# Down-projection weights of a decoder layer: low parts by accumulating transfers, and in the second feed-forward high parts by casting transfers

## The chip, the cores and the metric

The kernel runs on one core of a Trainium2 chip. The metric is the device time in microseconds (us) of one execution; the median of the runs is compared. TensorE (PE) multiplies matrices, VectorE (DVE), ScalarE (ACT) and GpSimd (POOL) work element by element, SyncE (SP) and GpSimd issue DMA transfers.

## The reference, cut to what matters

A decoder layer for 512 tokens of width 1024: a half-step feed-forward (f1), a mixer with attention and a convolution, a second half-step feed-forward (f2), and a gated embedding. Everything is float32. The part that the change touches is `w_down` of the two feed-forwards, 2816 x 1024 each:

```python
def swiglu(h, w_gu, w_down):
    g, u = jnp.split(h @ w_gu, 2, axis=-1)
    return (jax.nn.silu(g) * u) @ w_down

x = x + 0.5 * swiglu(rmsnorm(x, ffn1_norm[i]), ffn1_wgu[i], ffn1_wdown[i])
... # mixer
x = x + 0.5 * swiglu(rmsnorm(x, ffn2_norm[i]), ffn2_wgu[i], ffn2_wdown[i])
```

## The kernel before, in words

**Split products.** TensorE multiplies in the rounded format fp32r. To keep float32's accuracy, each operand is split into a high part (the value rounded to fp32r) and a low part (what the rounding left out), and `mm3` sums three products: low weight by high data, high by high, high weight by low data, in this order. So the first matmul of a tile reads the low weight part.

**Weight pieces.** `piece` fetches one 128 x 1024 piece of weights (512 KB; 128 x 768 and 384 KB in the last down-projection of each feed-forward): SyncE loads it into a buffer of the class `raw`, ScalarE rounds it into one of the class `hi`, and `split_into` has VectorE (or GpSimd, for some mixer weights) subtract, raw minus high, into one of the class `lo`. There are three buffers of each class (`SLOTS`), shared by all weights of the program.

**A feed-forward.** The 22 blocks of 128 hidden channels (`KF`) are made first plainly (4 of them in f1, 2 in f2: `products`), then in pairs (`pair`). A pair takes seven products of half-width matmuls (256 columns); the weights of some are sums of raw pieces (`f_s`), formed by VectorE or GpSimd. In f1 (`own=True`) the split weights of these sums have buffers of their own; in f2 they take `hi` and `lo` buffers too. The products of a pair stand in the order 1 and 2, 6 and 5, 7 and 3, then 4, each with a g group and a u group of 12 matmuls. After 8, 16 and 22 blocks `down` runs: for each of 8 output tiles one piece of `w_down` and 24 matmuls of 512 columns (18 in the last), then two VectorE operations that scale the tile and add it to x. In the profile the down-projection's tiles are `f_d`, its weights `raw_wd`, `whi_wd` and `wlo_wd`; in the order of instructions `f2_d0_3` is output tile 3 of f2's first down-projection, and `wd2` the weights of f2, `wd1` those of f1.

**What sets the order.** `record` writes the program down as operations without an order between engines. `passes` then lets `simulate`, a planner with a cost for each operation, place them in time, several times over, with the due times that `deadlines` takes from the pass before; `simulate` also gives out the buffers, and may start one of the next ten groups of matmuls (`WINDOW`) when the first in line isn't ready. `hybrid_layer` emits the operations in the order found. On the chip each engine runs its own list strictly in that order, and an instruction whose operands aren't ready, or whose buffer isn't free, holds up all that stand behind it on its engine. GpSimd issues no transfer in the kernel before.

Of the kernel before, what the change touches and what calls it, by code (L numbers as in the profile page):

```python
# [9 lines left out]
F32 = mybir.dt.float32  # L10
F32R = mybir.dt.float32r
I32 = mybir.dt.int32
AF = mybir.ActivationFunctionType
ALU = mybir.AluOpType
AX = mybir.AxisListType

P = 128
# [16 lines left out]
PIECE = 1024  # L34
# [14 lines left out]
MARGIN = 0.0  # L49

CAPS = {"cz": 2, "ct": 4}
FLEX = ("wkv", "wq", "wzc", "wzg", "wap")

class VT:


    def __init__(self, name, shape, dtype, cls):
# [5 lines left out]
        self.late = False  # L65
        self.kind = name[:2] if name[:2] in CAPS else None

# [142 lines left out]

class Op:
    __slots__ = (
        "i eng home flex what a k writes reads cost lat preds succs group ls npred start end vts done lock fset dma outs"
    ).split()


# [10 lines left out]
class Program:  # L227
    def __init__(self):
        self.ops, self.groups, self.tiles = [], [], []
        self.cur = self.behind = None  # L230
        for name, eng in (("tensor", "PE"), ("vector", "DVE"), ("scalar", "ACT"), ("gpsimd", "POOL"), ("sync", "SP"), ("flex", "FLEX")):
            setattr(self, name, Engine(self, eng))
# [13 lines left out]
    def add(self, eng, what, a, k):  # L246
        op = Op()
        op.flex = eng == "FLEX"
        eng = "DVE" if op.flex else eng
# [47 lines left out]
    def costs(self, op, eng=None):  # L297

        ins = op.reads
        o = op.writes[0] if op.writes else None  # L300
        n = max([v.free() for v in ([o] if o else []) + ins])
        psum = any(v.vt.cls == "ps" for v in op.writes + ins)
        eng = eng or op.eng
        op.lock = eng == "POOL"
        op.fset = None
        op.dma = 0.0
        vecs = sum(isinstance(v, V) for v in [*op.a[3:], *(v for n, v in op.k.items() if n != "accum_out")])
        if eng == "PE":
            if op.what == "transpose":
                op.cost, op.lat = 0.112, 0.3  # L310
            else:
                n = op.a[2].free()
                if op.a[2].vt.dtype == F32R:
                    op.cost, op.lat = (0.2272, 0.3) if n > 256 else (0.1197, 0.3)
                else:
                    op.cost, op.lat = max(0.15, n * 0.00167), 0.35
        elif eng == "DVE":
            op.lat = 0.15
            if op.what == "tensor_tensor":
                op.cost = 0.065 + n * 1.055e-3  # L320
            elif op.what == "scalar_tensor_tensor":
                op.cost = 0.08 + n * 1.12e-3
            elif op.what == "tensor_tensor_reduce":
                op.cost = 0.28 + n * 1.02e-3
            elif op.what in ("reduce_sum", "tensor_reduce"):
                op.cost = 0.08 + n * 1.03e-3
            else:
                op.cost = 0.08 + n * (1.25e-3 if psum else 0.9e-3)
            op.lock = not psum and op.what not in ("tensor_tensor_reduce", "reduce_sum", "tensor_reduce", "reciprocal")
        elif op.what == "dma_start" and eng == "ACT":  # L330
            op.cost, op.lat = 0.5, 2.6
        elif eng == "ACT":
            op.cost, op.lat = 0.07 + n * 0.88e-3, 0.17
            op.cost += 0.094 * vecs
            if "accum_out" in op.k:
                op.cost += 0.1
            f = op.a[2].name if len(op.a) > 2 else "Copy"
            op.fset = SETS.get(f)
        elif eng == "POOL":
            op.lat = 0.15  # L340
            if op.what == "tensor_tensor":
                op.cost = 0.14 + n * 2.1e-3
            elif op.what == "tensor_scalar":
                op.cost = 0.25 + n * 0.8e-3
            else:
                op.cost = 0.12 + n * 1.0e-3
        else:
            op.cost, op.lat = 0.47, 0.0
            v = (op.writes + op.reads)[0]
            op.dma = v.free() * v.shape[0] * 4 / 240e3  # L350
# [16 lines left out]
def deadlines(prog, when):  # L367

    end = max(when.values()) + 12.0
    gend = {}  # L370
    for g in prog.groups:
        gend[g] = when[g.ops[-1]] + g.ops[-1].cost
    for op in reversed(prog.ops):
        if op.eng == "PE":
            ls = when[op]
        else:
            ls = end
            for v in op.reads:
                if v.vt.cls == "ps" and not v.vt.name.startswith("cz"):
                    for o, w in op.preds.items():  # L380
                        if o.eng == "PE" and w:
                            ls = min(ls, gend[o.group] + (24.0 if v.vt.late else 5.0))
        for s in op.succs:
            d = s.ls
            if s.preds[op] and not s.eng == op.eng == "PE":
                d -= op.lat + (1.8 + op.dma if op.eng == "SP" else 0.0)
            ls = min(ls, d - op.cost)
        if op.outs and op.outs[0].cls in ("hi", "lo"):
            ls -= MARGIN
        op.ls = ls  # L390


WINDOW = 10


def simulate(prog, slots):

    free = {c: deque(range(n)) for c, n in slots.items()}
    inuse = dict.fromkeys(CAPS, 0)
    ready = {e: [] for e in ENGINES}  # L400
    busy = dict.fromkeys(ENGINES, 0.0)
# [17 lines left out]
    def push(t, kind, x=None):  # L419
        nonlocal seq  # L420
        heapq.heappush(events, (t, seq, kind, x))
        seq += 1
# [7 lines left out]
    dma_free = 0.0  # L430
# [5 lines left out]
    def can(op, slack):  # L436
        for vt in op.outs:
            if vt.slot is None:
                break
        else:  # L440
            return True
        need = {}
        for v in op.writes:
            vt = v.vt
            if vt.slot is None:
                need.setdefault(vt.cls, {})[vt] = True
        for c, vts in need.items():
            spare = 0
            if c == "a":
                if slack > 400.0:  # L450
                    return False
                spare = 0 if slack < 2.0 else 1 if slack < 6 else 3 if slack < 20 else 6
            if slack > LEAD.get(c, 1e9):
                return False
            if len(free[c]) < len(vts) + spare:
                return False
            if any(vt.kind and inuse[vt.kind] >= CAPS[vt.kind] for vt in vts):
                return False
        return True

    def launch(op, t):
        nonlocal dma_free, aset, lock_dve, lock_pool
        for v in op.writes:
            vt = v.vt
            if vt.slot is None:
                vt.slot = free[vt.cls].popleft()
                if vt.kind:
                    inuse[vt.kind] += 1
        c = op.cost
        if op.eng == "ACT" and op.fset and op.fset != aset:  # L470
            c += 1.28
            aset = op.fset
        if op.lock and op.eng == "DVE":
            c += max(0.0, lock_pool - t)
            lock_dve = t + c
        elif op.lock:
            c += max(0.0, lock_dve - t)
            lock_pool = t + c
        op.start = t
        busy[op.eng] = t + c  # L480
        if op.eng == "SP":
            dma_free = max(t + 0.6, dma_free) + op.dma
            op.end = dma_free + 1.5
        else:
            op.end = t + c + op.lat
        push(t + c, "wake")
        push(op.end, "done", op)
        for s in op.succs:
            if s.eng == op.eng != "PE" and s.npred == 1 and s.ls + lag - t < 6.0:
                hold[op.eng] = op.end  # L490
                if op.eng == "DVE" and s.lock:
                    hold["POOL"] = op.end + 0.1
# [4 lines left out]
    def pe(t):  # L497

        nonlocal cur, pos, lag
        while True:  # L500
# [18 lines left out]
            pick = None  # L519
            for n, g in enumerate(pending[:WINDOW]):  # L520
                off, ok = 0.0, True
# [27 lines left out]
    while left:  # L549
# [3 lines left out]
        t = events[0][0]  # L553
        while events and events[0][0] <= t + 1e-9:
            _, _, kind, x = heapq.heappop(events)
# [17 lines left out]
        for e in ENGINES:  # L573
# [29 lines left out]
            op = best[1]  # L603
# [48 lines left out]
def record():  # L652
    nc = Program()
# [41 lines left out]

    def piece(key, i, n=PIECE, off=0, cuts=1):

        raw = nc.tile(f"raw_{key}{i}", [P, PIECE], F32, "raw")
        hi = nc.tile(f"whi_{key}{i}", [P, PIECE], F32R, "hi")
        lo = nc.tile(f"wlo_{key}{i}", [P, PIECE], F32R, "lo")  # L700
        for c in range(cuts):
            s = slice(c * n // cuts, (c + 1) * n // cuts)
            d = slice(off + s.start, off + s.stop)
            nc.sync.dma_start(raw[:, s], Dram(key)[i][:, d])
            split_into(hi[:, s], lo[:, s], raw[:, s], eng=nc.flex if key in FLEX else nc.vector)
        return hi, lo
# [773 lines left out]
    for o in range(KD):  # L1480
# [4 lines left out]
        n = S // 2 if o == KD - 1 else S  # L1485
        for c in range(0, S, n):
            v = slice(c, c + n)
# [134 lines left out]
```

## Time and profile before

| | |
|---|---|
| time, median of 2 runs | 1173.55 us (1172.52 and 1174.57) |
| span of the profiled execution, first to last instruction | 1172.4 us |
| TensorE busy | 1161.6 us, 99% |
| VectorE busy | 973.4 us, 83% |
| ScalarE busy | 639.7 us, 55% |
| GpSimd busy | 456.2 us, 39% |
| granted TensorE clock, mean | 0.999 |
| moved by SyncE's queue | 114.12 MB |

The profile gives the span of one execution. The median of the runs lies 1.1 us above it; the profiled execution's own time beside the span isn't given apart. A row of a group of instructions reads: line, engine, operation, output <- inputs with their shapes, x count, then busy time in us, mean ns of one, and the engine's idle time just before them with what ended it. A row of waits reads: waiting engine and tile <- releasing engine and tile, us in total, times, longest. All operations are emitted by one line, so rows are told apart by the names of tiles.

### The profile page before, as it was taken

The numbers are of one execution on the slowest core, as the hardware profiler recorded it, in microseconds if no ns is written. First come the engines' busy times: TensorE is split into PE (matmuls) and PEld (weight loads), VectorE is DVE, ScalarE is ACT, GpSimd is POOL, SyncE is SP. The second block draws the span as 40 slices with busy tenths as digits, with TensorE's granted clock in tenths as the row PEclk, the third lists the DMA queues.
The fourth block names the chain that finished last, engine by engine and source line by source line (L and its number), as shares of the span: only waits on it lengthen the run. The fifth ranks groups of instructions, "written<-read, shape, count | busy, mean of one in ns | idle before, by whom it ended". The sixth has DMA issues, their size and how long they took to land.

```text
span 1172.4 us, 17962 instructions
## 1 busy us (share of the span) xinstructions
PE 1161.6 (99%) x6740; PEld 1029.6 (88%) x6740; DVE 973.4 (83%) x1481; ACT 639.7 (55%) x1139; POOL 456.2 (39%) x418
## 2 busy tenths in 40 slices
PE   9999999999999999999999999999999999999998
PEld 7898899889988888878888888889988999899886
DVE  8995799679886898999999786678966997599885
ACT  8552455335545579979865573545541555245542
POOL 2430465033303987887898600104402440122000
PEclk9999999999999999999999999999999999999999
DMA  7422323342233221312223233332333223331331
GB/s 226 146 85 96 126 75 106 99 136 76 82 104 100 90 91 37 108 55 72 76 89 106 88 94 93 105 96 102 107 104 132 74 86 100 121 127 41 104 108 72
DMA packets 37815, 115.30 MB, mean 98 GB/s; under 512 B 4704, under 2 KB 9440, under 8 KB 37728
## 3 DMA queue, kind: packets, MB, share of 16 engines
q1 hardware_dynamic: 37584, 114.12, 31.0%
q8 instruction: 53, 0.87, 0.3%
q14 instruction: 34, 0.28, 0.1%
q10 hardware_dynamic: 144, 0.03, 0.0%
HBM read 112.04 MB, written 2.10 MB: 97 GB/s over the span
## 4 chain that ended last, share of the span: by engine, by line
PE 94%; ACT 2%; DVE 2%; POOL 1%; issue 1%; DMA 0%; SPq 0%; DVEq 0%; ACTq 0%
PE f_d L1522 20%; PE ap L1522 4%; PE ga L1522 4%; PE pg L1522 4%; PE cp L1522 4%; PE wo L1522 4%; PE ca L1522 3%; PE gb L1522 3%; PE cb L1522 3%; PE f_u L1522 2%; PE f_g L1522 2%; PE q1b L1522 2%; PE q0b L1522 2%; PE sc L1522 2%; PE f_u14b L1522 1%; PE f_u20b L1522 1%
## 5 line engine op out<-in xcount | busy, mean ns | idle before, releaser
L1522 POOL TENSOR_TENSOR f_s<-raw_wgu,raw_wgu 128x512 f32<-128x512 f32 x51 | 86.6, 1710 | 345.5 <-DMA raw_wgu<-in_wgu 115.6
L1522 POOL TENSOR_TENSOR y<-y,ct 128x507 f32<-128x507 f32 (+27 forms) x90 | 119.1, 1343 | 6.2 <-ACT ct L1522 4.6
L1522 ACT ACTIVATE whi_wgu<-raw_wgu 128x1024 fp32r<-128x1024 f32 (+1 forms) x93 | 76.2, 834 | 81.5 <-PE f_d L1522 29.5
L1522 DVE TENSOR_TENSOR wlo_wgu<-raw_wgu,whi_wgu 128x1024 fp32r<-128x1024 f32 (+1 forms) x93 | 105.1, 1140 | 7.8 <-ACT whi_wgu L1522 7.3
L1522 DVE SCALAR_TENSOR_TENSOR cz<-u,dww,cz 128x504 f32<-128x504 f32 (+25 forms) x145 | 104.7, 732 | 2.3
L1522 ACT ACTIVATE whi_wd<-raw_wd 128x1024 fp32r<-128x1024 f32 (+1 forms) x48 | 47.4, 987 | 103.9 <-PE f_d L1522 84.6
L1522 DVE TENSOR_TENSOR f_d<-f_d,f_n_rb 128x512 f32<-128x512 f32 x48 | 33.4, 697 | 75.8 <-PE f_d L1522 75.8
L1522 DVE TENSOR_TENSOR f_wl<-f_s,f_wh 128x512 fp32r<-128x512 f32 x72 | 71.4, 1012 | 1.5 <-ACT f_wh L1522 1.0
L1522 POOL TENSOR_TENSOR f_s<-raw_wgu,f_s 128x512 f32<-128x512 f32 x31 | 52.3, 1694 | 51.6 <-DVE f_us L1522 20.6
L1522 DVE TENSOR_TENSOR wlo_wgu<-f_s,whi_wgu 128x512 fp32r<-128x512 f32 x80 | 66.3, 863 | 6.0 <-ACT whi_wgu L1522 5.8
L1522 ACT ACTIVATE whi_wgu<-f_s 128x512 fp32r<-128x512 f32 x80 | 46.6, 625 | 32.4 <-PE f_d L1522 8.9
L1522 ACT ACTIVATE ct<-u,dww 128x505 f32<-128x505 f32 (+28 forms) x90 | 58.2, 701 | 2.2 <-DVE u L1522 2.1
L1522 ACT ACTIVATE f_wh<-f_s 128x512 fp32r<-128x512 f32 x72 | 43.6, 626 | 26.6 <-DVE f_s L1522 12.9
L1522 POOL TENSOR_TENSOR f_s<-f_s,raw_wgu 128x512 f32<-128x512 f32 x31 | 49.2, 1594 | 20.8 <-DVE f_s L1522 6.0
L1522 DVE TENSOR_TENSOR wlo_wd<-raw_wd,whi_wd 128x1024 fp32r<-128x1024 f32 (+1 forms) x48 | 54.1, 1128 | 3.8 <-ACT whi_wd L1522 3.6
L1522 ACT ACTIVATE f_gs<-f_gs 128x512 f32<-128x512 f32 x44 | 27.6, 629 | 34.8 <-DVE f_gs L1522 34.4
L1522 POOL TENSOR_TENSOR f_t<-x 128x256 f32<-128x256 f32 x8 | 6.5, 807 | 86.8 <-DVE x L1522 81.6
L1522 DVE SCALAR_TENSOR_TENSOR x<-f_d,x 128x512 f32<-128x512 f32 x48 | 32.9, 689 | 1.4
L1522 DVE TENSOR_TENSOR f_s<-raw_wgu,raw_wgu 128x512 f32<-128x512 f32 x25 | 32.9, 1319 | 0.0
L1522 ACT ACTIVATE s<-s,m,q_r 128x128 f32<-128x128 f32 x64 | 31.0, 491 | 0.5 <-DVE m L1522 0.4
L1522 ACT ACTIVATE whi_wzc<-raw_wzc 128x1024 fp32r<-128x1024 f32 x16 | 17.0, 1061 | 22.3 <-issue 8.4
L1522 ACT ACTIVATE whi_wzg<-raw_wzg 128x1024 fp32r<-128x1024 f32 x16 | 17.1, 1069 | 16.9 <-PE ga L1522 5.0
(1621 smaller groups left out, 4525.3 us busy)
## 6 DMA issues: line engine op xcount, KB each, us to landing
raw_wgu<-in_wgu SPq DMA_DIRECT2D x80, 512.0 KB, 3.7
raw_wd<-in_wd SPq DMA_DIRECT2D x32, 512.0 KB, 3.5
raw_wzc<-in_wzc SPq DMA_DIRECT2D x16, 512.0 KB, 3.6
raw_wzg<-in_wzg SPq DMA_DIRECT2D x16, 512.0 KB, 3.6
raw_wd<-in_wd SPq DMA_DIRECT2D x16, 384.0 KB, 3.1
raw_wgu<-in_wgu SPq DMA_DIRECT2D x32, 128.0 KB, 2.9
raw_wq<-in_wq SPq DMA_DIRECT2D x8, 512.0 KB, 3.6
raw_wap<-in_wap SPq DMA_DIRECT2D x8, 512.0 KB, 3.6
```

The source lines that it names most:

```text
L1522: getattr(engines[op.eng], op.what)(*a, **k)
```

## The change

For the weights of the two down-projections `piece` no longer subtracts. In f1 the piece is loaded and rounded as before; ScalarE then writes the negated high part into the low buffer, and a transfer issued by GpSimd adds the piece from HBM onto it once more, so that low = weight - high. In f2 there is no raw piece: a transfer issued by GpSimd rounds it on the way into the high buffer, and the low part follows as in f1. So a down weight of f2 crosses from HBM twice, both times by GpSimd's queue, one of f1 once by SyncE's and once by GpSimd's. The planner gets a cost for GpSimd's transfers. It also gets a rule for all weights: a piece is given one of the three `hi` (or `lo`) buffers only when it is among the next in the order in which TensorE will use them (`turns`).

```diff
+ADD_ISSUE, ADD_RATE = 1.2, 120e3
+BY_DMA = {"wd1": True, "wd2": False}
...
+        elif eng == "POOL" and op.what == "dma_start":
+            op.cost, op.lat, op.lock = ADD_ISSUE, 0.0, False
+            v = op.writes[0]
+            op.dma = v.free() * v.shape[0] * 4 / (ADD_RATE if "accum_op" in op.k else 240e3)
...
+            if c in TURNS and any(vt not in turns[c][: len(free[c])] for vt in vts):
+                return False
...
+        elif op.dma:
+            dma_free = max(t + c, dma_free) + op.dma
+            op.end = dma_free + 2.0
...
     def piece(key, i, n=PIECE, off=0, cuts=1):
 
+        d = slice(off, off + n)
+        if key in BY_DMA:
+            hi = nc.tile(f"whi_{key}{i}", [P, PIECE], F32R, "hi")
+            lo = nc.tile(f"wlo_{key}{i}", [P, PIECE], F32R, "lo")
+            if BY_DMA[key]:
+                raw = nc.tile(f"raw_{key}{i}", [P, PIECE], F32, "raw")
+                nc.sync.dma_start(raw[:, 0:n], Dram(key)[i][:, d])
+                nc.scalar.activation(hi[:, 0:n], raw[:, 0:n], AF.Copy)
+            else:
+                nc.gpsimd.dma_start(hi[:, 0:n], Dram(key)[i][:, d])
+            nc.scalar.activation(lo[:, 0:n], hi[:, 0:n].bitcast(F32), AF.Copy, scale=-1.0)
+            nc.gpsimd.dma_start(lo[:, 0:n], Dram(key)[i][:, d], accum_op=ALU.add)
+            return hi, lo
```

The planner's order moves with it. Three places follow, all in f2's first down-projection.

On GpSimd, where before only the sums for the next pair (blocks 8 and 9) stood between the sums of block 6 and those of block 10:

```order
L1522 TENSOR_TENSOR f2_s3_6_1_8843<-raw_wgu26_01_8565,f2_s1_6_1_8712 128x512
L1522 TENSOR_TENSOR f2_s0_8_0_9252<-raw_wgu28_10_9224,raw_wgu28_11_9147 128x512
L1522 TENSOR_TENSOR f2_s2_8_0_9265<-raw_wgu28_00_9158,raw_wgu28_10_9224 128x512
L1522 TENSOR_TENSOR f2_s1_8_1_9282<-f2_s0_8_1_9258,raw_wgu28_00_9158 128x512
L1522 TENSOR_TENSOR f2_s3_8_0_9297<-raw_wgu28_01_9191,f2_s1_8_0_9270 128x512
```

Now on GpSimd at the same place (a transfer to `whi` casts, one to `wlo` adds):

```order
L1557 DMA whi_wd20_8995<-in_wd2 128x1024
L1557 DMA whi_wd21_9015<-in_wd2 128x1024
L1557 DMA whi_wd22_9045<-in_wd2 128x1024
L1557 DMA wlo_wd20_9049<-in_wd2 128x1024
L1557 DMA wlo_wd21_9053<-in_wd2 128x1024
L1557 DMA wlo_wd22_9056<-in_wd2 128x1024
L1557 DMA whi_wd23_9088<-in_wd2 128x1024
L1557 DMA whi_wd24_9121<-in_wd2 128x1024
L1557 DMA wlo_wd23_9118<-in_wd2 128x1024
L1557 DMA whi_wd25_9152<-in_wd2 128x1024
L1557 DMA wlo_wd24_9149<-in_wd2 128x1024
L1557 DMA wlo_wd25_9181<-in_wd2 128x1024
```

Twelve transfers have come ahead of the next pair's sums, and the first add stands behind the third cast, the add of piece 3 behind the cast of piece 4.

On ScalarE, before, at the end of the same down-projection and the first weight of the next pair:

```order
L1522 ACTIVATE whi_wd25_9139<-raw_wd25_9059 128x1024
L1522 ACTIVATE whi_wd26_9174<-raw_wd26_9090 128x1024
L1522 ACTIVATE whi_wd27_9207<-raw_wd27_9123 128x1024
L1522 ACTIVATE whi_wgu28_1_9240<-raw_wgu28_00_9158 128x1024
L1522 ACTIVATE whi_wgu28_2_9280<-raw_wgu28_01_9191 128x1024
```

Now on ScalarE, from the negation of piece 4 on:

```order
L1557 ACTIVATE wlo_wd24_9149<-whi_wd24_9121 128x1024
L1557 ACTIVATE wlo_wd25_9181<-whi_wd25_9152 128x1024
L1557 ACTIVATE whi_wgu28_1_9189<-raw_wgu28_00_9106 128x1024
L1557 ACTIVATE whi_wgu28_2_9250<-raw_wgu28_01_9133 128x1024
L1557 ACTIVATE whi_wgu28_6_9301<-f2_s1_8_0_9239 128x512
L1557 ACTIVATE whi_wgu28_6_9301<-f2_s1_8_1_9232 128x512
L1557 ACTIVATE wlo_wd26_9315<-whi_wd26_9271 128x1024
```

Two weights of the next pair have moved ahead of pieces 6 and 7, and stand behind the negation of piece 5.

On TensorE, before, from the end of output tile 3 of this down-projection:

```order
L1522 MATMUL f2_d0_3_9135<-f2_a01h_8820,wlo_wd23_9082 128x512
L1522 MATMUL f2_d0_3_9135<-f2_a01h_8820,whi_wd23_9073 128x512
L1522 MATMUL f2_d0_3_9135<-f2_a01l_8900,whi_wd23_9073 128x512
L1522 MATMUL f2_d0_4_9170<-f2_a00h_8360,wlo_wd24_9115 128x512
L1522 MATMUL f2_d0_4_9170<-f2_a00h_8360,whi_wd24_9106 128x512
```

Now on TensorE at the same place:

```order
L1557 MATMUL f2_d0_3_9156<-f2_a01h_8941,wlo_wd23_9118 128x512
L1557 MATMUL f2_d0_3_9156<-f2_a01h_8941,whi_wd23_9088 128x512
L1557 MATMUL f2_d0_3_9156<-f2_a01l_8958,whi_wd23_9088 128x512
L1557 MATMUL f2_g8b_9194<-f2_h0_h_7767,wlo_wgu28_1_9192 128x256
L1557 MATMUL f2_g8b_9194<-f2_h0_h_7767,whi_wgu28_1_9189 128x256
```

Groups of 12 half-width matmuls of the next pair (`f2_g8b`, `f2_u8b` and others) now stand between output tiles 3 and 4, 4 and 5, and more of them between 5 and 6 and between 6 and 7. f2's second down-projection is arranged like the first. In f1's first two, such groups stand after tile 4, after 5 and after 6 (the group g8a of the pair after the first down-projection comes after tile 5 and one other group). The third down-projection of each feed-forward has none in between.

More of the change, by code (lines that the diff above doesn't have):

```diff
@@ L212 @@
     __slots__ = (
-        "i eng home flex what a k writes reads cost lat preds succs group ls npred start end vts done lock fset dma outs"
+        "i eng home flex what a k writes reads cost lat use preds succs group ls npred start end vts done lock fset dma outs"
     ).split()
@@ L385, in deadlines @@
             if s.preds[op] and not s.eng == op.eng == "PE":
-                d -= op.lat + (1.8 + op.dma if op.eng == "SP" else 0.0)
+                d -= op.lat + (1.8 + op.dma if op.dma else 0.0)
             ls = min(ls, d - op.cost)
@@ L390, in deadlines @@
         op.ls = ls
+        op.use = when[op] if op.eng == "PE" else min((s.use for s in op.succs if s.preds[op]), default=end)
 WINDOW = 10
+TURNS = ('hi', 'lo')
 def simulate(prog, slots):
     free = {c: deque(range(n)) for c, n in slots.items()}
+    first = {}
+    for op in prog.ops:
+        for vt in op.outs:
+            if vt.cls in TURNS and vt not in first:
+                first[vt] = op.use, op.i
+    turns = {c: sorted((k, vt.name, vt) for vt, k in first.items() if vt.cls == c) for c in TURNS}
+    turns = {c: [vt for _, _, vt in ts] for c, ts in turns.items()}
     inuse = dict.fromkeys(CAPS, 0)
@@ L466, in launch @@
                 vt.slot = free[vt.cls].popleft()
+                if vt.cls in TURNS:
+                    turns[vt.cls].remove(vt)
                 if vt.kind:
```

## The prediction

> **What bounds the kernel now.** I read the shares by engine first, then TensorE's waits, then the stretches.
>
> ```profile
> PE 1161.6 (99%) x6740; PEld 1029.6 (88%) x6740; DVE 973.4 (83%) x1481; ACT 639.7 (55%) x1139; POOL 456.2 (39%) x418
> ```
> ```profile
> PE sc L1522 <- DVE qT_l L1522: 2.0, 1, 2.0
> PE warm L1522 <- DVE ones L1522: 1.1, 1, 1.1
> PE f_u L1522 <- ACT f_n_rb L1522: 0.7, 1, 0.7
> PE f_g2a L1522 <- ACT f_gs L1522: 0.6, 1, 0.6
> PE ple_sp L1522 <- DVE ple_dgl L1522: 0.6, 1, 0.6
> PE f_g L1522 <- DVE wlo_wgu L1522: 0.2, 1, 0.2
> PE kTp L1522 <- POOL zk L1522: 0.2, 1, 0.2
> ```
> These are all of TensorE's waits: 5.4 us of 1172.4. No relief of another engine can give back more than that, under 0.5%, and no row names a down-projection. The stretches say the same (f1's first down-projection, its second and third pairs, f2's first and last down-projection; first the stretch and its length, then each engine's busy time):
>
> ```profile
> 93.00:137.00 44.00, 44.00 (x198) 36.50 (x197) 26.24 (x27) 12.58 (x16) 9.30 (x6) 1.00 0.32 104
> 137.00:217.00 80.00, 80.00 (x668) 79.90 (x667) 75.37 (x107) 43.16 (x77) 36.41 (x22) 1.00 0.31 102
> 862.00:906.00 44.00, 44.00 (x199) 36.50 (x198) 27.29 (x31) 9.67 (x11) 6.83 (x4) 1.00 0.44 140
> 1090.00:1123.00 33.00, 33.00 (x149) 27.41 (x148) 28.08 (x40) 17.57 (x25) 0.00 (x0) 1.00 0.42 122
> ```
> TensorE is full in all of them at clock 1.00, though VectorE is at 94% in the second. In the chain that ended last a down-projection is one unbroken piece:
>
> ```profile
> 862.01 43.55 PE f_d L1522 x192
> 1090.54 32.67 PE f_d L1522 x144
> ```
> 43.55 / 192 = 0.227 us a matmul, so an output tile takes 24 x 0.227 = 5.44 us, in the last down-projection 18 x 0.227 = 4.08. The question is only whether the new weight chain can deliver a pair every 5.44 (4.08) us.
>
> **What the change removes.** VectorE loses 48 subtractions:
>
> ```profile
> L1522 ACT ACTIVATE whi_wd<-raw_wd 128x1024 fp32r<-128x1024 f32 x32 | 33.9, 1058 | 86.7 <-PE f_d L1522 84.6 <-PE f_u6b L1522 1.3 <-ACT whi_wd L1522 0.4
> L1522 ACT ACTIVATE whi_wd<-raw_wd 128x768 fp32r<-128x768 f32 x16 | 13.5, 846 | 17.2 <-issue 16.4 <-ACT whi_wd L1522 0.5 <-PE f_u20b L1522 0.2
> L1522 DVE TENSOR_TENSOR wlo_wd<-raw_wd,whi_wd 128x1024 fp32r<-128x1024 f32 x32 | 38.9, 1216 | 2.9 <-ACT whi_wd L1522 2.9
> L1522 DVE TENSOR_TENSOR wlo_wd<-raw_wd,whi_wd 128x768 fp32r<-128x768 f32 x16 | 15.2, 951 | 0.9 <-ACT whi_wd L1522 0.7
> ```
> 38.9 + 15.2 = 54.1 us off VectorE, worth 0 since TensorE never waited there. ScalarE gains 24 negations in f1 (about 1 us each); in f2 they replace the 24 roundings. SyncE loses 24 loads, GpSimd's queue gains 72 transfers. All that is off the path; only latency counts.
>
> **What the new transfers take** stands nowhere in this trace, where GpSimd issues none. The nearest rows are SyncE's loads (size in KB, us from issue to landing):
>
> ```profile
> raw_wd<-in_wd SPq DMA_DIRECT2D x32, 512.0 KB, 3.5
> raw_wd<-in_wd SPq DMA_DIRECT2D x16, 384.0 KB, 3.1
> ```
> 128 KB more cost 0.4 us, so 512 KB are 1.6 us of moving on 1.9 fixed. The *cast* moves as much; I add 1.0 us for GpSimd's issue (its shortest 128x512 add is 1.29 us, in a row below) and take Tc = 4.5 us (4.1 for 384 KB). The *add* also reads its destination: twice the moving, 1.9 + 3.2 + 0.9 = 6.0 = Ta (1.9 + 2.4 + 0.9 = 5.2). Lower end for both: the plain 3.5 and 3.1. Upper end: two us for the issue, and thrice the moving for the add: Tc 5.5 (4.9), Ta 1.9 + 4.8 + 2.0 = 8.7 (7.6). I stay nearer the loads.
>
> The Trainium skill, page "DMA: Bandwidth & Descriptors", section "Anatomy of one DMA — SWDGE (gpsimd) path", fits a GpSimd transfer as 2.0 us + bytes/436e3, an estimate of 3.2 us for 512 KB; with that for both, the sum would be about that of the first rival. No run before this one shows it.
>
> **f2, where the chain lies open.** Three buffers each hold high and low parts, and f2's pairs use the same ones, so a first down weight gets a buffer only when a pair's last products release it (ScalarE, then TensorE's last pair matmul and first down matmul):
>
> ```profile
> 857.94 1.04 ACT L1522 ACTIVATE whi_wd<-raw_wd 128x1024 fp32r<-128x1024 f32 x1
> 859.21 1.06 ACT L1522 ACTIVATE whi_wd<-raw_wd 128x1024 fp32r<-128x1024 f32 x1 [0.23 <-ACT whi_wd L1522]
> 862.20 1.04 ACT L1522 ACTIVATE whi_wd<-raw_wd 128x1024 fp32r<-128x1024 f32 x1
> 867.56 1.06 ACT L1522 ACTIVATE whi_wd<-raw_wd 128x1024 fp32r<-128x1024 f32 x1 [3.46 <-PE f_d L1522]
> ```
> ```profile
> 860.40 0.28 PE L1522 MATMUL f_u6b<-f_t_h,wlo_wgu 128*128 128x256 f32 x1
> ...
> 861.72 0.28 PE L1522 MATMUL f_u6b<-f_t_l,whi_wgu 128*128 128x256 f32 x1
> 861.84 0.40 PE L1522 MATMUL f_d<-f_a00h,wlo_wd 128*128 128x512 f32 x1
> ```
> Buffers came 3.9 and 2.6 us before the first down matmul and 0.4 after it; a tile's release reaches ScalarE 0.2 to 0.3 us after the tile. Today 1.06 + 1.2 us fit. Let E be the time at which the first down matmul would start:
> - Start: cast 0 goes at -3.9, lands at 0.6, its negation ends at 1.8 (two hops of 0.1). On GpSimd the first add stands behind the third cast, which waits for E; it goes at 1.8 and lands at 7.8. The tile's first matmul reads the low part: **7.8 us** of wait.
> - Tiles 0 to 2 run to 24.1. Cast 3 can go when tile 0 is done (13.2), lands at 17.9, is negated at 19.1; its add stands behind cast 4, which waits for tile 1 (18.7) and is issued by 19.7; it lands about 25.4: **1.3 us**. Tile 3 ends at 30.8.
> - TensorE's order then has the next pair's g8b. Its high part stands on ScalarE behind negation 5 (30.0) and takes the buffer that tile 3 frees: 0.2 + 1.06 + 1.2 and hops, **2.7 us**. Add 4 is there by 31, add 5 by 36.
> - Tiles 6 and 7 stand among the pair's products and hold one buffer each through cast, negation and add, so the pair turns over two. A product is 24 x 0.12 = 2.9 us and a new weight about 2.7; where two products are interleaved some 1.3 us are missing. I take **2.0 us** (0 to 7). GpSimd's adds for this pair (next row) wait behind add 5, and are used from tile 5 on; VectorE's freed time covers them. Without that cover, it is one such add, 1.8 us.
>
> ```profile
> L1522 POOL TENSOR_TENSOR f_s<-raw_wgu,raw_wgu x2: 1293/1780/2267, 895.4 to 896.7; 128x512 f32<-128x512 f32 x2
> ```
> That is 13.8 us, twice 27.6. The third down-projection has smaller pieces and no pair to fill in. By the same steps with 4.1, 0.85 and 5.2: 6.4 at the start, 2.4 at tile 3, 2.2 at tile 6, 1.1 at tile 7 (its negation stands behind wgate0's rounding), **12.1 us**.
>
> The third starts like the first two (its first rounding 4.0 us ahead: the first row below, against the last). f1 stands otherwise (the second row; its down-projection starts at 93.0):
>
> ```profile
> 1086.42 0.83 ACT L1522 ACTIVATE whi_wd<-raw_wd 128x768 fp32r<-128x768 f32 x1
> ...
> 77.35 1.06 ACT L1522 ACTIVATE whi_wd<-raw_wd 128x1024 fp32r<-128x1024 f32 x1 [1.01 <-PE f_u6b L1522]
> ```
> ```profile
> 1090.38 0.40 PE L1522 MATMUL f_d<-f_a20h,wlo_wd 128*128 128x512 f32 x1
> ```
> **f1, where it is covered.** The pair's middle weights have buffers of their own, so the first rounding stood 15.6 us ahead. In the stride: tile ends, 0.2 + rounding 1.06 + negation 1.06 + hops 0.2 + Ta 6.0 = 8.5 us, against two tiles = 10.9. The cover goes above Ta = 8.4. What is left is g8a after tile 5 of the first one: its buffer is tile 5's, 2.7 us after it, and one group of 1.4 us lies between: **1.3 us**; in the second a whole tile lies between. The transfer engines have room: 0.32 x 44 = 14 us now, plus 8 adds x 3.2 = 26, gives 40 of 44 us and more.
>
> The mixer's order shifts a little; its waits before sum to 2.8 us (rows sc, ple_sp and kTp), so I put nothing on it.
>
> **The sum**, against the profiled execution's span: 27.6 + 12.1 + 1.3 = 41.0; 1172.4 + 41.0 = 1213.4. The median of the runs lies 1.1 us above the span: **1214.5 us**, 3.5% slower.
>
> **The rivals.**
> 1. *GpSimd's transfers are as short as SyncE's.* Tc = Ta = 3.5 (3.1): 4.4 + 0 + 2.7 + 0 in each of two, 4.6 in the third (3.4 at the start, 1.2 at tile 7), 1.3 in f1: 20.1 us, 1194, which a measurement of 2% can't tell from no change. For it: the same bytes over the same engines, under half busy. Against: an add reads twice. From 41.0 to 20.1 as Tc + Ta falls from 10.5 to 7.0 is 6 us per us; it decides below Tc + Ta = 7.6, where the loss is 23.5 us. Chance 0.17.
> 2. *Adds or issues are slower.* Tc 5.5, Ta 8.7: starts of 11.5, 4.7 at tile 3, 2.7, and 5 in the pair: 23.9 twice; 9.6 + 5.5 + 5.5 in the third; 5 in f1, now past its cover: 73 us, 1247. For it: GpSimd's add above takes 1.29 to 2.27 us for one shape, so something holds that engine up at times. Against: VectorE, which would be the likeliest, is busy for only 27.29 of 44 us there. Chance 0.2. The Trainium skill, page "SBUF — State Buffer", section "SBUF: two separate sides", has a rule that speaks for it: while VectorE runs in a two-port mode, GpSimd can't write a transfer's descriptors. No trace shows it yet.
> 3. *VectorE was the hidden limit*, and 54 us less of it shorten the pair stretches. It would give at most the 5.4 us of waits, 1168. Against: TensorE is at 80.00 of 80.00 there. Chance 0.03.
>
> The forecast has the other 0.6, with its own range 1202 to 1235. The range for 8 in 10 takes in part of both big rivals: 1188 to 1252. Within 2% is 1150 to 1197, what a measurement of this kernel can't tell from no change: 0.18, from rival 1 and what is left of 3; faster by over 2%: 0.01; slower 0.81.
>
> **What would show it.** TensorE's waits list, empty of f_d now, names DMA wlo_wd, most of it at three places, each where f2 passes from pairs to a down-projection, 6 to 10 us a time. f1's down-projections stay within 3 us of 43.55 and 32.67 us. Landing times of whi_wd near 4.5 and of wlo_wd near 6.0 would bear out the sizes. VectorE falls to about 920 us busy with no gain. I am wrong if f2's first down matmul follows the pair within 3 us, or if f1 waits as much as f2.

## The result, and the profile after

The changed kernel takes **1265.48 us** (median of two runs, 1265.32 to 1265.64), 1.0778 times the time before, 95% interval 1.0754 to 1.0801. The forecast was 1214.5 us with a range up to 1252: the direction was right, the time lies outside the range. The profiled execution has a span of 1263.8 us, 91.4 more than before, at a mean granted clock of 0.976. In experiments 9 and 10 one execution took 1.9 and 2.4 times as long as the others; the ratios leave these out.

The shares by engine, after:

```profile
PE 1188.6 (94%) x6740; PEld 1041.9 (82%) x6740; DVE 925.0 (73%) x1424; ACT 665.6 (53%) x1165; POOL 523.9 (41%) x499
```

Start from TensorE, which was at 99%. Its matmuls are the same 6740, so the span's 91.4 us split exactly in two: idle time rose from 10.8 us (1172.4 - 1161.6) to 75.2 (1263.8 - 1188.6), that is by **64.4**, and the *same* matmuls were busy for **27.0** us longer. The forecast had only idle time in its sum, 41.0 us. VectorE is at 925.0 us, 48.4 less, with no gain.

TensorE's waits after (total, times, longest):

```profile
PE f_d L1557 <- DMA wlo_wd<-in_wd: 40.4, 10, 10.6
PE kTp L1557 <- POOL zk L1557: 3.6, 1, 3.6
PE ple_sp L1557 <- DVE ple_dgh L1557: 3.5, 1, 3.5
PE f_g8b L1557 <- DVE wlo_wgu L1557: 3.4, 1, 3.4
PE f_g16b L1557 <- DVE wlo_wgu L1557: 3.4, 1, 3.4
PE q1b L1557 <- DVE of L1557: 2.0, 1, 2.0
```

The first row is the one that the prediction had named. Rows 2, 3 and 6 are in the mixer, whose code the change does not touch. The stretches say where (start and end, length, then busy time of each engine, and the granted clock behind POOL): f1's three down-projections; f2's first pairs (with the last 2.7 us of the mixer's `wo`), then f2's three down-projections with the pairs between them; and, in a fence of its own, the mixer to the end of `cp`.

```profile
93.50:145.00 51.50, 49.90 (x243) 41.93 (x242) 22.36 (x27) 21.08 (x25) 14.60 (x12) 1.00 0.65 151
221.20:272.60 51.40, 49.66 (x243) 41.73 (x242) 24.14 (x28) 21.75 (x26) 15.43 (x12) 1.00 0.69 163
327.30:360.90 33.60, 33.14 (x148) 26.97 (x147) 20.96 (x30) 20.85 (x29) 10.00 (x8) 1.00 0.76 169
799.00:888.60 89.60, 87.58 (x623) 82.21 (x621) 76.73 (x120) 44.16 (x77) 31.39 (x21) 1.00 0.31 102
888.60:947.20 58.60, 42.37 (x171) 34.28 (x170) 13.93 (x19) 8.98 (x9) 13.19 (x15) 0.83 0.58 136
947.20:1038.50 91.30, 89.79 (x697) 86.91 (x695) 75.92 (x110) 46.16 (x83) 34.29 (x24) 1.00 0.33 97
1038.50:1091.20 52.70, 38.03 (x171) 31.04 (x170) 16.58 (x20) 9.18 (x10) 14.39 (x15) 0.90 0.65 153
1091.20:1161.40 70.20, 69.23 (x529) 66.65 (x527) 55.05 (x86) 35.12 (x63) 18.74 (x15) 1.00 0.32 87
1161.40:1214.40 53.00, 39.31 (x147) 31.32 (x146) 22.07 (x32) 17.62 (x25) 10.32 (x14) 0.84 0.59 121
```
```profile
360.80:758.20 397.40, 384.34 (x1781) 318.43 (x1780) 328.19 (x546) 268.56 (x515) 259.51 (x284) 0.98 0.27 81
```

The mixer's stretch in the profile before, for comparison:

```profile
354.00:733.80 379.80, 376.98 (x1781) 314.97 (x1780) 329.42 (x550) 264.81 (x513) 253.44 (x280) 1.00 0.28 85
```

Length less TensorE's busy time is its idle time. f2 (rows 4 to 9 of the first fence): 2.0 + 16.2 + 1.5 + 14.7 + 1.0 + 13.7 = 49.1 us. f1's down-projections: 1.6 + 1.7 + 0.5 = 3.8. The mixer: 13.06 after against 2.82 before, 10.2 more, and 7.4 us more of busy time for the same 1781 matmuls. f2, from the end of `wo` (801.7 us) to the gated embedding, has 18.5 us more of busy time (363.5 against 345.0) for the same matmuls; the other 1.1 us are f1's. f2's three down-projections are also the stretches whose granted clock is 0.83, 0.90 and 0.84 instead of 1.00.

The trace's record of the granted clock has it at 0.50 ("the half clock" below) for 13.7 us of the mixer and 47.8 us of f2. TensorE was busy in 12.4 and 28.2 of these; half of that, 20.3 us, is an estimate of what the slow clock took. The other 6.7 of the 27.0 us stand beside a granted clock of 1.00, some of them around short waits (f1's 1.5 us from its first down-projection on); they were not taken apart.

Last, the transfers (size, us from issue to landing):

```profile
wlo_wd<-in_wd POOLq DMA_DIRECT2D x32, 512.0 KB, 7.3
whi_wd<-in_wd POOLq DMA_DIRECT2D x16, 512.0 KB, 4.0
wlo_wd<-in_wd POOLq DMA_DIRECT2D x16, 384.0 KB, 5.6
```

### The profile page after: what moved, and what is told of

Read it like the earlier page. It is cut to its first block, busy times and chain, and to the rows that moved or that the text cites. A ratio compares the mean times of both kernels' runs of the same rounds, so it can differ in the third digit from the quotient of the medians.

```text
span 1263.8 us, 17980 instructions
## 1 busy us (share of the span) xinstructions
PE 1188.6 (94%) x6740; PEld 1041.9 (82%) x6740; DVE 925.0 (73%) x1424; ACT 665.6 (53%) x1165; POOL 523.9 (41%) x499
## 4 chain that ended last, share of the span: by engine, by line
PE 70%; DVE 10%; issue 8%; ACT 5%; DMA 4%; POOL 2%; SPq 0%; DVEq 0%; POOLq 0%; ACTq 0%
PE f_d L1557 13%; PE cp L1557 4%; PE pg L1557 3%; PE ap L1557 3%; PE wo L1557 3%; PE gb L1557 3%; PE ga L1557 3%; DMA wlo_wd<-in_wd 3%; PE cb L1557 3%; DVE wlo_wgu L1557 2%; PE ca L1557 2%; PE f_u L1557 2%; PE f_g L1557 2%; PE q0b L1557 2%; DVE cz L1557 2%
## 5 line engine op out<-in xcount | busy, mean ns | idle before, releaser
L1557 POOL DMA_DIRECT2D wlo_wd<-in_wd x48 | 42.1, 877 | 181.3 <-ACT wlo_wd L1557 145.1
L1557 POOL TENSOR_TENSOR y<-y,ct 128x511 f32<-128x511 f32 (+22 forms) x90 | 113.2, 1273 | 3.0 <-ACT ct L1557 1.0
L1557 DVE SCALAR_TENSOR_TENSOR cz<-u,dww,cz 128x510 f32<-128x510 f32 (+24 forms) x145 | 100.5, 729 | 0.8
L1557 ACT ACTIVATE wlo_wd<-whi_wd 128x1024 fp32r<-128x1024 f32 (+1 forms) x48 | 47.3, 984 | 61.1 <-DMA whi_wd<-in_wd 57.1
L1557 POOL DMA_DIRECT2D whi_wd<-in_wd x24 | 13.5, 561 | 143.8 <-PE f_d L1557 81.3
L1557 ACT ACTIVATE ct<-u,dww 128x511 f32<-128x511 f32 (+23 forms) x90 | 58.6, 701 | 0.1
L1557 ACT ACTIVATE whi_wd<-raw_wd 128x1024 fp32r<-128x1024 f32 (+1 forms) x24 | 23.7, 989 | 41.4 <-PE f_d L1557 39.1
L1557 PE MATMUL f_d<-f_a20h,wlo_wd 128*128 128x512 f32 x64 | 27.9, 435 | 14.1 <-DMA wlo_wd<-in_wd 14.1
L1557 PE MATMUL f_d<-f_a00h,wlo_wd 128*128 128x512 f32 x64 | 27.3, 426 | 13.2 <-DMA wlo_wd<-in_wd 13.2
L1557 PE MATMUL f_d<-f_a10h,wlo_wd 128*128 128x512 f32 x64 | 26.1, 408 | 13.1 <-DMA wlo_wd<-in_wd 13.1
```

The costliest lines, as they stand in the source:

```text
L1557: getattr(engines[op.eng], op.what)(*a, **k)
```

## The experiments

Ratios are to the kernel before, run on the same chip, with 95% intervals. The first four take the change apart.

**1. The buffer rule alone.** No weight goes by GpSimd's transfers; only `turns` is left of the change.

```diff
-BY_DMA = {"wd1": True, "wd2": False}
+BY_DMA = {}
```


> The change's buffer rule alone: BY_DMA is empty, so all down weights are loaded, rounded and subtracted as before, but buffers are given in the order of use. Its mixer has the same order of matmuls as the changed kernel. Theory: that order, not the transfers, made the mixer 14.8 us longer (423.3 to 438.1), so about 1188 us, f1 and f2 as before. Rival: the transfers' load on GpSimd and on the DMA engines did it, so within 3 us of 1173.5.

Measured 1193.52 us, 1.0170 (1.0153 to 1.0187): 20 us from a rule that moves not one byte, and more than the 1188 expected. Its two longest waits and its stretch of the mixer:

```profile
PE kTp L1557 <- POOL zk L1557: 4.2, 3, 3.7
PE ple_sp L1557 <- DVE ple_dgh L1557: 3.5, 1, 3.5
```
```profile
354.70:751.40 396.70, 383.31 (x1781) 317.52 (x1780) 327.52 (x546) 268.69 (x515) 259.97 (x284) 0.99 0.26 81
```

16.9 of the 20 us are here (396.70 against 379.80), most of the rest in f2 (2.4 us). The first thing that moved is a group of 24 matmuls. On TensorE, before, ahead of the keys' transposition `kTp`:

```profile
388.44 0.39 PE L1522 MATMUL cb<-mix_h_l,whi_wzc 128*128 128x512 f32 x1
388.68 0.38 PE L1522 MATMUL kTp<-ident,zk 128*128 128x128 f32 x2
```

This group `cb` (24 x 0.227 = 5.4 us) used to stand between the keys' projection and `kTp` and covered GpSimd's rotation of the keys, `zk`; with the rule it comes later, a group `ca` stands ahead of `kTp`, and TensorE waits there. Here is that place in the changed kernel (start, duration, what, idle time before it):

```profile
389.77 0.39 PE L1557 MATMUL ca<-mix_h_l,whi_wzc 128*128 128x512 f32 x1
393.79 1.80 PE L1557 MATMUL kTp<-ident,zk 128*128 128x128 f32 x4 [3.63 <-POOL zk L1557]
```

That is one wait of several. Groups of `q1b`, `sc`, `ga`, `ap` and `e` stand elsewhere too, and the waits at `ple_sp` and `q1b` have places of their own; which move made which of them was not taken apart.

**2. f1's part and the rule.** f2's weights are subtracted as before.

```diff
-BY_DMA = {"wd1": True, "wd2": False}
+BY_DMA = {"wd1": True}
```


> Only f1's down weights by adding transfers, f2 as before. Theory: the stages add up: 14.8 for the mixer's order and 6.7 for f1, about 1195 us, f2 as before (346 us). Rival (the transfers disturb what follows): over 1200.

Measured 1199.72 us, 1.0223 (1.0208 to 1.0238): about 6 us above the rule alone, and 5 above the 1195 expected; f2 is 2.4 us longer here too, as with the rule alone, which the theory had left out.

**3. f2's part and the rule.** f1's weights are subtracted as before.

```diff
-BY_DMA = {"wd1": True, "wd2": False}
+BY_DMA = {"wd2": False}
```


> Only f2's down weights by casting and adding transfers, f1 as before. Theory: f2 is 70 us longer by itself and the mixer 15, about 1258 us. Rival, f2's loss partly comes from what f1's change left behind: under 1245.

Measured 1259.63 us, 1.0737 (1.0719 to 1.0756): 66 us above the rule alone, as expected. The parts add up: 20 for the rule, 6 for f1 and 66 for f2 give 1266 us.

**4. f2's high parts by load and rounding.** The casts go, the adds stay.

```diff
-BY_DMA = {"wd1": True, "wd2": False}
+BY_DMA = {"wd1": True, "wd2": True}
```


> f2's high parts not by casting transfers but as in f1: loaded early by SyncE, rounded by ScalarE; low parts still by adding transfers in both. Theory: two transfers in series behind a buffer that comes free 4 us ahead make f2's loss. With one of them gone the start falls from 10.6 and 10.0 us to about 6, in the third from 6.4 to about 4, the waits at tile 3 go, those beside the pair's weights stay at 1 to 3: f2 loses about 30 instead of 70, about 1227 us. Rival, the adding transfers alone are too slow for the stride: f2 loses 60 or more, over 1250.

Measured 1231.24 us, 1.0489 (1.0474 to 1.0505). A raw piece has a buffer of its own class, so its load runs ahead of the release of a `hi` buffer; the cast can't. f_d's waits are half of the changed kernel's 40.4 us:

```profile
PE f_d L1557 <- DMA wlo_wd<-in_wd: 20.0, 7, 6.7
```

The three starts wait 6.7, 5.9 and 5.0 us (about 6, 6 and 4 were expected), and at tile 3 no wait over 0.3 us is left.

**5. The rule kept away from the mixer.** The changed kernel, but the mixer's weights do not enter `turns`. TensorE's order in the mixer is then the one before.

```diff
-            if vt.cls in TURNS and vt not in first:
+            if vt.cls in TURNS and vt not in first and not any(n in vt.name for n in ('_wzc', '_wzg', '_wq', '_wkv', '_wap', '_wple')):
...
-            if c in TURNS and any(vt not in turns[c][: len(free[c])] for vt in vts):
+            if c in TURNS and any(vt in turns[c] and vt not in turns[c][: len(free[c])] for vt in vts):
...
-                if vt.cls in TURNS:
+                if vt in turns.get(vt.cls, ()):
```


> The changed kernel with the buffer rule (turns) applied to the weights of the feed-forwards only; the mixer's weights take buffers as before the change. Theory (the rule moved the mixer's matmuls, and that alone cost it about 15 us, cp behind it 2.5 us by the clock): the stage from the keys' and values' projection to cp goes back from 351.5 to about 336 us, cp from 46.0 to 43.5, f2 stays as in the changed kernel: 1246 to 1250 us. Rival (the mixer is slower because of the transfers or of the state in which f1 leaves the queues): no change, 1263 to 1267 us.

Measured 1237.60 us, 1.0534 (1.0511 to 1.0557). The mixer's stretch:

```profile
356.70:738.20 381.50, 378.67 (x1781) 316.10 (x1780) 330.26 (x550) 265.08 (x513) 253.48 (x280) 1.00 0.27 84
```

397.40 has gone to 381.50, idle 2.8 as before. For the mixer the theory holds, but the gain is 28 us in all, not the 15 to 19 expected: the planner's order behind and ahead of the mixer changed as well, f1's stages became 3.7 us shorter and f2's 6.4 (the profiled execution). Which rows of the order did that was not taken apart.

**6. The same, with f1's part only**, and **7. with f1's part and f2's adds.** Both are experiment 5 with another `BY_DMA`, the first and the second of these lines:

```diff
-BY_DMA = {"wd1": True, "wd2": False}
+BY_DMA = {"wd1": True}
+BY_DMA = {"wd1": True, "wd2": True}
```

> As e5_turns_ff, and f2's down weights loaded and subtracted as before the change, so that only f1's low parts come by adding transfers. Theory (f1's part costs 5 to 6 us, the rule on the feed-forwards 2 to 3 us in f2's first pairs, the mixer nothing): 1179 to 1184 us. Rival (f1's adding transfers disturb the mixer too): 1190 us and more.

Measured 1177.82 us, 1.0022 (1.0010 to 1.0034): f1's adding transfers cost 0.2%, about 2.6 us. Its whole row for the down-projections:

```profile
PE f_d L1557 <- DMA wlo_wd<-in_wd: 0.4, 1, 0.4
```

> As e5_turns_ff, with f2's down weights loaded raw by SyncE and rounded by ScalarE like f1's, so that only the low parts come by adding transfers. Theory (the terms add up: the 1231 us of the same kernel with the rule on all weights less the mixer's 17 to 20 us): 1210 to 1215 us. Rival (the mixer's loss and f2's hide each other in part): 1220 us and more.

Measured 1202.92 us, 1.0241 (1.0218 to 1.0264), 8 to 12 us better than expected. As in experiment 5 the planner's order changed outside the mixer: by the profiled executions f1 is 3.7 and f2 6.7 us shorter than in experiment 4. With it the change stands as a ladder:

| step | ratio | added, of 1173.55 us |
|---|---|---|
| f1: adds, and the rule on the feed-forwards (6) | 1.0022 | 2.6 |
| f2: adds (7) | 1.0241 | 25.7 |
| f2: casts for loads and roundings (5) | 1.0534 | 34.4 |
| the rule on the mixer's weights (the change) | 1.0778 | 28.6 |

None of the steps gives anything back, and no version is faster than the kernel before. The planner orders the whole program anew at each step, so what a step adds depends on the others: the rule costs 20 us when it comes first, 28.6 with its part on the mixer's weights last.

**8. TensorE kept busy through f2's waits.** This asks where the 27.0 us of longer busy time come from. Ahead of f2's three down-projections stand 40, 40 and 24 matmuls of ones whose results nobody reads, and 10 and 14 ahead of tiles 3 and 6 of the third; `nc.behind` makes the planner place them behind the matmul recorded just before. The order is otherwise unchanged.

```diff
+KEEP = {(0, 0): 40, (8, 0): 40, (16, 0): 24, (16, 3): 10, (16, 6): 14}
...
+                if tag == "f2" and (k0, o) in KEEP:
+                    keep = ps_tile(f"{tag}_keep{k0}_{o}")
+                    nc.behind = next(op for op in reversed(nc.ops) if op.eng == "PE")
+                    with nc.group(f"{tag}_keep{k0}_{o}"):
+                        for _ in range(KEEP[k0, o]):
+                            nc.tensor.matmul(keep, ones_r, h[0][0], start=True, stop=True)
+                    nc.behind = None
```


> The changed kernel with groups of 40, 40, 24, 10 and 14 matmuls of ones, whose results nobody reads, put on TensorE ahead of the matmuls of f2's down-projections that wait longest; the order is otherwise the same. Theory (waits longer than about 3.4 us make the granted clock fall to 0.5 for a while, and f2's matmuls take longer for it): the first real matmul of each down-projection comes when it did, the granted clock in f2 goes from 0.83 to 0.90 back to about 1.00, and the time falls by 8 to 18 us to 1247 to 1258 us. Rival (the matmuls behind the waits are slow for another reason, such as weights that come late): no change or a little longer, 1264 to 1270 us.

Measured 1258.34 us, 1.0708 (1.0692 to 1.0724): *more* work, and 8 us less time (0.0070 x 1173.55), at a mean granted clock of 0.991 instead of 0.976. The first matmuls of f2's first down-projection, in the changed kernel:

```profile
899.38 0.79 PE L1557 MATMUL f_d<-f_a00h,wlo_wd 128*128 128x512 f32 x1 [10.58 <-DMA wlo_wd<-in_wd]
899.97 0.63 PE L1557 MATMUL f_d<-f_a00h,whi_wd 128*128 128x512 f32 x1
900.39 0.63 PE L1557 MATMUL f_d<-f_a00l,whi_wd 128*128 128x512 f32 x1
900.82 0.63 PE L1557 MATMUL f_d<-f_a00h,wlo_wd 128*128 128x512 f32 x1
```
and with the filled wait:
```profile
895.95 0.50 PE L1565 MATMUL f_d<-f_a00h,wlo_wd 128*128 128x512 f32 x1 [1.27 <-DMA wlo_wd<-in_wd]
896.29 0.39 PE L1565 MATMUL f_d<-f_a00h,whi_wd 128*128 128x512 f32 x1
896.52 0.40 PE L1565 MATMUL f_d<-f_a00l,whi_wd 128*128 128x512 f32 x1
```

Read the starts: 0.42 to 0.43 us apart after a wait of 10.58, 0.23 apart after one of 1.27. The matmuls themselves run at half speed behind a long wait. Without the 128 extra ones, TensorE's busy time is 9.9 us less than in the changed kernel (the first row's 1208.6 less the second's 29.9 is 1178.7):

```profile
PE 1208.6 (96%) x6868; PEld 1058.3 (84%) x6868; DVE 920.5 (73%) x1424; ACT 665.4 (53%) x1165; POOL 522.4 (42%) x499
```
```profile
L1565 PE MATMUL f_keep<-f_h_h,ones_r 128*128 128x512 f32 x128 | 29.9, 390 | 0.0
```

Not all of the gain is the filling's. The profiled execution is 8.6 us shorter than the changed kernel's: 5.4 us in f2, whose half clock fell from 47.8 to 13.7 us, 2.4 in the mixer, where nothing was filled and the half clock lasted 6.8 instead of 13.7 us, and the rest in f1. So about 5 us are what the filling brought, and part of its gain turned into waiting. The place is tile 3 of the second down-projection, where the changed kernel waited 1.39 us:

```profile
1060.13 0.79 PE L1565 MATMUL f_d<-f_a10h,wlo_wd 128*128 128x512 f32 x1 [3.74 <-DMA wlo_wd<-in_wd]
```

TensorE got there sooner, the piece did not, and behind this wait the clock fell again.

**9. Transfers that write instead of adding.** This leaves the addition out, so the low parts are the weights themselves, and asks what the add costs by itself.

```diff
-            k = {n: real(v) for n, v in op.k.items()}
+            k = {n: real(v) for n, v in op.k.items() if n != "accum_op"}
```


> The changed kernel in the same order, with the transfers onto the negated high parts writing instead of adding (the low parts are then the weights themselves: the addition is left out). Theory (an add holds the transfer engines longer than a cast and takes 5.6 us alone against a cast's 4.0, and the queue works off one transfer behind another): the landing of wlo_wd falls from 7.3 to 4 to 5.5 us, the starts of f2's down-projections wait 7 to 8, 7 to 8 and 4 to 5 us instead of 10.6, 10.0 and 6.4, and the whole takes 1238 to 1252 us. Rival (adding costs nothing, several transfers in GpSimd's queue are what takes the time): landings stay at 7 to 9 us at the starts, 1262 to 1268 us.

Measured 1251.46 us, 1.0667 (1.0646 to 1.0689), 13 us less (0.0111 x 1173.55).

```profile
wlo_wd<-in_wd POOLq DMA_DIRECT2D x32, 512.0 KB, 4.8
```
```profile
PE f_d L1557 <- DMA wlo_wd<-in_wd: 23.7, 7, 7.3
```

The landing falls from 7.3 to 4.8 us and f2's longest wait from 10.6 to 7.3; the other two starts wait 6.5 and 4.7 us instead of 9.9 and 6.4. The rival, that adding costs nothing, falls.

**10. The third cast behind the first two adds.** Experiment 5, with one wish to the planner for piece 2 of each of f2's down-projections. In the changed kernel GpSimd issues three casts, then three adds (start, duration of the issue, what, idle time before it):

```profile
885.03 0.62 POOL L1557 DMA_DIRECT2D whi_wd<-in_wd  x1 [11.82 <-DVE f_us L1557]
886.23 0.54 POOL L1557 DMA_DIRECT2D whi_wd<-in_wd  x1 [0.59 <-PE f_u6a L1557]
889.10 0.53 POOL L1557 DMA_DIRECT2D whi_wd<-in_wd  x1 [2.33 <-PE f_u6b L1557]
891.19 0.89 POOL L1557 DMA_DIRECT2D wlo_wd<-in_wd  x1 [1.56 <-ACT wlo_wd L1557]
```

What the transfer engines did in that wait (888 to 900 us; the queue, packets, MB, share of the 16 engines):

```profile
q0 software_dynamic: 622, 2.24, 88.7%
...
wlo_wd<-in_wd POOLq DMA_DIRECT2D x3, 512.0 KB, 8.9
whi_wd<-in_wd POOLq DMA_DIRECT2D x1, 512.0 KB, 4.9
```

GpSimd's queue alone keeps all 16 engines 88.7% busy, so the transfers stand in line. By the trace the third cast lands at 893.97, the first add (issued at 891.19) at 899.33, the second at 901.78, the third at 904.26: 2.5 us from one to the next, and the cast that the third tile needs goes ahead of the add that the first tile needs.

```diff
+                if i == 2:
+                    nc.behind = next(o for o in reversed(nc.ops) if "accum_op" in o.k and o.outs[0].name == f"wlo_{key}0")
                 nc.gpsimd.dma_start(hi[:, 0:n], Dram(key)[i][:, d])
+                nc.behind = None
```


> The kernel with the rule on the feed-forwards' weights only (e5_turns_ff), and in each down-projection of f2 the third piece's casting transfer is issued behind the first two adds instead of ahead of them. Theory (GpSimd's transfers move one behind another, so the cast ahead of the first add delays its landing by its own 2 to 2.5 us): the first add lands 5.5 to 6.5 us after its issue instead of 7.8, each start waits about 2 us less, and the time falls from 1237.6 to 1228 to 1234 us. Rival (an add is slow whenever others are in flight, ahead of it or behind it): the starts wait as before, the third tile comes later, 1237 to 1243 us.

Measured 1232.53 us, 1.0501 (1.0484 to 1.0519), about 4 us less than experiment 5 (0.0033 x 1173.55). The two intervals overlap a little, and TensorE's, VectorE's, ScalarE's and GpSimd's orders in f2 changed in other places too, so the 4 us alone don't show the mechanism. The trace of one more execution, which took 1229.2 us, shows it.

> The same kernel as e10_cast_behind, for a profile at the usual speed. Theory: the first add of each down-projection of f2 lands 5.5 to 6.5 us after its issue, and the three starts wait about 8, 8 and 5 us. Rival: 7.5 us and more from issue to landing, starts of 10, 10 and 6.8.

```profile
860.94 0.53 POOL L1560 DMA_DIRECT2D whi_wd<-in_wd  x1 [0.83 <-PE f_u6a L1560]
865.90 0.89 POOL L1560 DMA_DIRECT2D wlo_wd<-in_wd  x1 [4.43 <-ACT wlo_wd L1560]
867.40 0.88 POOL L1560 DMA_DIRECT2D wlo_wd<-in_wd  x1 [0.61 <-ACT wlo_wd L1560]
867.95 0.88 POOL L1560 DMA_DIRECT2D whi_wd<-in_wd  x1
```
```profile
PE f_d L1560 <- DMA wlo_wd<-in_wd: 32.3, 10, 8.0
```

The first add now lands at 871.47, 5.6 us after its issue, where in experiment 5's trace it took 7.75; the longest wait is 8.0 against 10.2, and the three starts are 8.0, 7.9 and 5.8 against 10.2, 10.1 and 6.8. Landing and starts come out as the theory had them, the third start 0.8 us above it.

## Why the prediction was wrong

Its mechanism held in part: the longest waits are where it put them, three at f2's starts, and f1's stride is covered. Its sum of 41.0 us missed 50.4 of the 91.4: f2's slower matmuls (18.5), the mixer (17.6: 10.2 of waits and 7.4 of slower matmuls), f2's waits (8.7 more than the sum had) and f1 (5.0 more); 0.6 are left over.

**The matmuls were counted at one speed.** Every tile in the sum is 24 x 0.227 us, "Tiles 0 to 2 run to 24.1" in the first down-projection. The profile before shows a granted clock of 1.00 up to its last 2 us, and its longest wait was 2.0 us; the prediction itself forecast waits of 6.4 to 7.8 us and did not ask what the clock does behind them. Measured: matmuls 0.43 us apart behind the 10.58 us wait, and 27.0 us more busy time in all, 18.5 in f2, 7.4 in the mixer with `cp` and 1.1 in f1; about 20 of the 27 are the half clock's. Experiment 8 shows the cause of f2's by filling the waits. The Trainium skill, page "TensorE: Matmul & The Clock Gate", section "What's actually happening", states that TensorE falls to half rate after at least one idle window of about 3.4 us. The rows of experiment 8 agree with it: half rate behind 10.58 us, full rate behind 1.27. The half clock behind a wait of 2.02 us in experiment 5, shown below, does not. It would have named the term, not its size.

**"The mixer's order shifts a little; its waits before sum to 2.8 us, so I put nothing on it."** This failed. Small waits say that the order there is tight, not that a shift is free. The rule alone costs 20 us, 16.9 of them in the mixer (experiment 1); taking the mixer's weights out of it gives back 28.6, 15.9 of them there (experiment 5). One group that had covered GpSimd's `zk` left its place, which is 3.6 of the mixer's 13.1 us of waits; what moved the others stays open.

**The start's add was mis-sized, because it isn't alone.** "It goes at 1.8 and lands at 7.8" took Ta = 6.0 us. An add with nothing ahead of it takes 5.6, so the size was fair; but the prediction put the third cast ahead of it only for GpSimd's issue, not for the transfer engines, and there it costs 2.2 us more (7.75 against 5.6 in experiments 5 and 10). In the changed kernel's first start the add went 2.4 us behind the last pair matmul instead of 1.8 and landed 8.1 us later instead of 6.0. The starts were 10.6 and 9.9 us instead of 7.8 twice; the third was 6.4 as forecast. In the rest, tile 3 measured 2.3 and 1.4 us for 1.3, and 2.8 in the third for 2.4; g8b and g16b 3.4 for 2.7; tile 6 of the third 4.6 for 2.2, tile 7 nothing for 1.1; the pairs' stretches behind the first two idle for 1.5 and 1.0 us for 2.0 each. All of f2's idle time is 49.1 us, 48.4 more than before, against the 39.7 (27.6 + 12.1) of the sum.

What was right, or nearly: Tc, 4.0 measured for 4.5 and 3.5 for the smaller piece's 4.1. f1's cover: its down-projections idle for 3.8 us against 1.3 (g8a 1.2 of it), and f1 as a whole is 6.3 us longer; 2.6 once the mixer's weights are out of the rule. VectorE's 48 us, worth nothing.

The rivals: the first (transfers as short as SyncE's) falls with landings of 5.6 and 7.3 us. The second (Ta 8.7, 1247 us) came nearest in time but not by its reason: it wanted every add to be that slow, which would have broken f1's cover too, and only the crowded ones are (8.1 to 9.1 in the first start). For its cause, GpSimd held up at its issues, the rows speak against it: the adds' issues take 0.85 to 1.04 us, in and out of the busy stretches, where it had put two. The third (VectorE was the limit) falls with f_d's waits.

## What to carry to other kernels

When a change will leave TensorE waiting for several us, price the wait twice: the gap, and the matmuls behind it that run at half speed; a kernel whose longest wait is 2.0 us can't show this in its own profile. A planner's rule that is meant for one stage belongs to that stage's buffers only: applied to all, it cost 20 us here without any of the transfers it was written for. And a chain of transfers on one queue is timed by what is ahead of it, so the transfer that the next matmul needs goes first.

## What the runs showed of the hardware that was not expected

- An accumulating transfer of 512 KB takes 5.6 us from issue to landing with nothing ahead of it, a casting one 4.0; several in the queue land 2.5 us apart while the 16 engines are 89% busy.
- The half clock comes in pieces of 3.4 us or multiples: in the changed kernel's trace 13.7 us from 891.5, 10.2 from 1041.7, 6.8 from 1164.6. It is not tied to a wait of 3.4 us. Behind this one of 2.02 us in experiment 5 eight matmuls started 0.43 us apart, while the same wait of 2.0 us before the change had none, and one of 3.35 us at `g16b` in the changed kernel had none either:

```profile
509.53 0.50 PE L1557 MATMUL sc<-kzh,qT_l 128*128 128x512 f32 x1 [2.02 <-DVE qT_l L1557]
...
510.81 0.63 PE L1557 MATMUL sc<-kzh,qT_h 128*128 128x512 f32 x1
511.23 0.63 PE L1557 MATMUL sc<-kzl,qT_h 128*128 128x512 f32 x1
```

  What decides between them was not tried; only that every wait of over 3.4 us brought it in the traces behind the ratios above. Nor is the size fixed: in seven executions with the same order in the mixer and the same two waits of about 3.5 us there, the half clock lasted 6.8 to 13.7 us in all.
